# A planned attention kernel with other costs in its planner, and the last pair of heads taken head by head

## The chip, the cores and the metric

The kernel runs on one core of a Trainium2 chip. The metric is the device time of one launch in microseconds (us), as the median of several executions. A profile is one execution recorded by the hardware profiler; its span runs from the first to the last instruction and is a little shorter than the device time of the same execution.

The engines' names in the profile: PE is TensorE (matrix multiplication), PEld its weight loads, ACT is ScalarE, DVE is VectorE, POOL is GpSimd, SP issues most of the DMAs.

## The reference

Softmax attention without a mask, batch 8, 8 heads, 512 rows, 64 columns:

```python
scores = np.einsum('bhqd,bhkd->bhqk', q, k) / np.sqrt(64)
attn = np.exp(scores - scores.max(axis=-1, keepdims=True))
attn = attn / attn.sum(axis=-1, keepdims=True)
return np.einsum('bhqk,bhkd->bhqd', attn, v)
```

Inputs and output are float32, 64 heads in all.

## The kernel before

**Pairs and groups.** Heads are taken in 32 pairs, g = 0 to 31. The scores of a head are computed transposed, keys on the partitions: a chunk c of 128 keys against all 512 queries is one block of 128x512, so a pair has eight blocks (g, c, h). The list `stream` gives the order of the blocks; two successive blocks make a group m, which lies in one PSUM tile `st` of 128x1024 (three such tiles, `ps_st`). Between the first and the last pair a group is chunk c of both heads, so that pair g holds groups 4g to 4g+3. The last group is split in two, so there are 129 groups, 0 to 128.

**Stages of a pair.** SP loads k, q and v in float32. GpSimd casts them to float16 (`qkp`, line 331, and `vp`, line 323; V has an added column of ones). PE transposes q and k (eight 128x128 transposes, line 348) into one of two PSUM banks (`ps_x`, tags x0 and x1), and VectorE copies them to `tqk` (line 355, "copy"). PE then computes a group's scores, two matmuls of depth 64 (line 374): head h sits on partitions 64h to 64h+63. ScalarE takes the exponential of the whole group into `pt` (line 379). The values of a head are computed in four units, each the sum over the four chunks for 128 queries (four matmuls of 65 columns, line 462); seven units share a bank `o`. When the seven are done VectorE normalises them (a reciprocal and a multiplication, lines 440 and 441, "norm") into `ring`, and SP stores the heads that are complete (line 449).

**Groups on VectorE.** Some groups' exponentials are computed on VectorE instead of ScalarE: first a "raise" reads the scores from PSUM into integers `z` (line 393), then six passes finish the exponential from SBUF (lines 406, 417 and four times 428).

**The order.** Each engine works its instructions in the order in which the program issues them, and that order is set when the kernel is built by the class `Plan`. It runs a clock in steps of 5 ns with booked costs (the constants ahead of `__init__`), in two parts:

- `step_pe` decides for PE. If the scores of the next group may start (a PSUM tile `st` is free and the pair's copy is done: `free`), and either those of the one after could too or ScalarE's booked work (`backlog`) is under HURRY, it issues scores. If the scores aren't due but will be within 150 ns and the backlog is small, it holds PE. Otherwise it issues transposes of the next pair if their data are booked as there (`ready_kq`) and a bank is free, or a unit of values (`values`), or scores after all.
- `step_dve` decides for VectorE. A raise, copy or normalisation that is due goes first, raises ahead of the others. If none is due, the next pass goes, unless a job already known falls due more than LATE before the end of the pass.

`for_dve` says whether a group goes to VectorE: not before group 6, not in the last three pairs, and only if no pass of the group before is still to be issued and no raise waits. `exps[m]` is the booked time at which group m's exponentials are there; `values` starts a head when all its groups are. Of the last head, the values of a chunk start when that chunk is there (`wants`, `last_values`, line 477), in a bank of their own.

The first three groups are issued by `first_pair`, outside the class; the constructor books their times. The step "feed" issues the loads of pair g+5 and the casts of pairs g+3 and g+2; it goes ahead of the first scores of pair g.

Of the kernel before, what the change touches and what calls it, by code (L numbers as in the profile page):

```python
# [12 lines left out]
EXP = mybir.ActivationFunctionType.Exp  # L13
# [3 lines left out]
class Plan:  # L17
# [10 lines left out]

    SLOT, EXP, EXP_DONE, EXP_FIXED = 216, 853, 1085, 51
    INTO, OUT_OF = 95, 105
    TRANSPOSE, V_UNIT = 225, 130
    TO_ACT, TO_DVE, TO_PE = 275, 210, 60
    COPY, NORM, NORM_COLUMN = 700, 380, 67
    RAISE, PASSES, LATE = 1216, (867, 822, 1400, 1400, 1400, 1372), 700
    HURRY = 1200
    STEP = 5
    FIRST_UNIT = 4

    def __init__(self, groups, pairs, first):
        self.groups, self.pairs = groups, pairs
        self.pe, self.act, self.dve = 6000, 4800 + first * 904, 5800
        self.m, self.tiled = first, True
        self.read = []
        self.exps = {}
        for m in range(first):
            self.exps[m] = 4800 + m * 904 + self.EXP_DONE
            self.read.append(self.exps[m])
        self.tq = {0: 5800}  # L50
        self.next_t = 1
        self.part_t = 0
        self.banks = [5100, 5800]
        self.todo = [(g, h) for g in range(pairs) for h in range(2)]
        self.head = None
        self.units = self.FIRST_UNIT
        self.member = {b: m for m, grp in enumerate(groups) for b in grp}
        self.ready = []
        self.passes = []
        self.steps = []  # L60

    def note(self, t, *what):
# [15 lines left out]
    def for_dve(self, m):  # L78
        g = self.groups[m][0][0]
        return (  # L80
            m > 5
            and g < self.pairs - 3
            and not self.passes
            and not any(x[1] == "raise" for x in self.ready)
        )

    def scores(self, t):
        m, grp = self.m, self.groups[self.m]
        slots = 2 if len(grp) == 2 and 0 < grp[0][0] and grp[0][2] == grp[1][2] else 1
        on_dve = self.for_dve(m)  # L90
        if m % 4 == 0 and grp[0][0] > 0 and len(grp) == 2:
            self.note(t, "feed", grp[0][0])
        self.note(t, "scores", m, on_dve)
        t += (0 if self.tiled else self.INTO) + self.SLOT * slots
        self.tiled = True
        if on_dve:
            self.ready.append((t + self.TO_DVE, "raise", (m,)))
            self.read.append(1e9)
        else:
            begin = max(self.act, t + self.TO_ACT)  # L100
            self.act = begin + self.EXP * len(grp) // 2 + self.EXP_FIXED
            self.exps[m] = self.act + self.EXP_DONE - self.EXP - self.EXP_FIXED
            self.read.append(self.exps[m])
        self.m += 1
        self.pe = t
# [61 lines left out]
    def step_pe(self, t):  # L167
        if self.m == len(self.groups):
            self.values(t)
            return  # L170
        g = self.groups[self.m][0][0]
        backlog = self.act - t
        one, two = self.free() <= t, self.free(1) <= t
        if one and (two or backlog < self.HURRY):
            return self.scores(t)
        if not one and backlog < 1300 and self.free() < t + 150:
            return
        if self.part_t:
            return self.transposes(t)
        if (  # L180
            self.next_t < self.pairs
            and self.next_t <= g + 1
            and t >= self.ready_kq(self.next_t)
            and self.bank(t) is not None
        ):
            return self.transposes(t)
        if not self.values(t) and one:
            self.scores(t)

    def step_dve(self, t):  # L190
        now = [x for x in self.ready if x[0] <= t]
        if now:
            job = min(now, key=lambda x: (x[1] != "raise", x[0]))
            self.ready.remove(job)
            _, kind, what = job
            self.note(t, kind, *what)
            if kind == "norm":
                self.dve = t + self.NORM + self.NORM_COLUMN * what[1]
                self.banks[what[2]] = self.dve + self.TO_PE
            elif kind == "copy":  # L200
                self.dve = t + self.COPY
                self.banks[what[1]] = self.tq[what[0]] = self.dve + self.TO_PE
            else:
                self.dve = t + self.RAISE
                self.read[what[0]] = self.dve + self.TO_PE
                self.passes += [(what[0], s) for s in range(len(self.PASSES))]
        elif self.passes:
            m, s = self.passes[0]
            if min((x[0] for x in self.ready), default=1e9) > t + self.PASSES[s] - self.LATE:
                self.passes.pop(0)  # L210
                self.note(t, "pass", m, s)
                self.dve = t + self.PASSES[s]
                if s == len(self.PASSES) - 1:
                    self.exps[m] = self.dve + self.TO_PE

    def run(self):
        t = 0
# [12 lines left out]
def kernel(  # L230
# [10 lines left out]
    NI = S // P  # L241
# [4 lines left out]
    LAST = NP - 1  # L246


    stream = []
    for g in range(NP):  # L250
        if g == 0:
            stream += [(g, c, h) for h in range(2) for c in range(NI)]
        elif g == LAST:
            stream += [(g, c, h) for c in range(2) for h in range(2)]
            stream += [(g, c, h) for h in range(2) for c in range(2, NI)]
        else:
            stream += [(g, c, h) for c in range(NI) for h in range(2)]
    groups = [stream[n : n + 2] for n in range(0, len(stream), 2)]
# [31 lines left out]
    first = {}  # L290
# [310 lines left out]
    with tc.manual_schedule():  # L601
        first_loads()
        load(1, "kq")
        load(0, "v")
        for g in range(2, 5):
            load(g, "kq")
            load(g - 1, "v")
        load(4, "v")
        make_identity(nc, ident)
        for n in range(NV):  # L610
            nc.vector.memset(vps[n][:, :, :, D : D + 1], 1.0)
        first_pair()
        cast_qk(1)
        cast_v(0)
        cast_qk(2)
        cast_v(1)
        feed(0)
        do = {
            "transposes": transposes,
            "scores": scores,  # L620
            "values": values,
            "feed": feed,
            "raise": raise_,
            "copy": lambda g, b: copy(g),
            "pass": pass_,
            "norm": lambda u, n, b: normalise(u, n),
        }
        for what, *args in Plan(groups, NP, 3).run():
            do[what](*args)
# [30 lines left out]
```

## Time and profile before

| What | Value |
|---|---|
| median of 5 executions | 123.27 us (122.89 to 124.48) |
| the profiled execution: device time | 123.39 us |
| its span | 121.6 us |
| busy time of PE / DVE / ACT / POOL | 107.7 / 99.6 / 114.3 / 74.7 us |
| granted TensorE clock | 0.999 |
| groups raised on VectorE | 6 |
| first DMA issue, last DMA issue | 0.73 and 118.94 us |

A row of the group table reads: line, engine, operation, out<-in by tile names, shapes, how many | busy time, mean ns of one | the engine's idle time just before them, and what ended most of it. A row of the timeline reads: start, length, engine, line, operation, how many were merged, and in brackets the idle time ahead and its releaser. The chain of waits is followed back from the last instruction to what released each.

### The profile page before, as it was taken

How to read it: one execution, taken by the hardware profiler on the slowest of the kernel's cores; microseconds unless marked ns; L12 is line 12 of the kernel's file. 1: busy time of each engine (PE TensorE's matmuls, PEld its weight loads, DVE VectorE, ACT ScalarE, POOL GpSimd, SP SyncE). 2: the span in 40 equal slices, each digit the busy share in tenths (PEclk: the TensorE clock that was granted, in tenths of full speed). 3: DMA queues.
4: the chain of work that ended last, by engine and by line, in shares of the span. 5: the costliest groups of instructions: out<-in, count | busy, mean ns of one | idle time of the engine just before them, and what ended most of it. 6: DMA issues, size and time to landing. Idle time of an engine off the chain costs nothing.

```text
span 121.6 us, 3951 instructions
## 1 busy us (share of the span) xinstructions
PE 107.7 (89%) x1557; PEld 67.2 (55%) x1557; DVE 99.6 (82%) x171; ACT 114.3 (94%) x127; POOL 74.7 (61%) x101
## 2 busy tenths in 40 slices
PE   7969788889899798998998998889999998999970
PEld 2636455547456455664566564656655665556550
DVE  1457899989999898699999899996979899976451
ACT  4699999999999999999999999999999999999970
POOL 2358979998699958396587981465955479200000
PEclk9999999999999999999999999999999999999999
DMA  4999999999999999996899998998999893313234
GB/s 116 289 334 382 381 380 384 383 319 302 356 362 330 325 328 340 319 339 237 248 302 286 308 321 281 279 328 264 312 322 334 286 314 102 102 49 127 91 113 152
DMA packets 35603, 33.82 MB, mean 278 GB/s; under 512 B 2688, under 2 KB 35584, under 8 KB 35584
## 3 DMA queue, kind: packets, MB, share of 16 engines
q1 hardware_dynamic: 35152, 33.24, 83.8%
q10 hardware_dynamic: 432, 0.33, 0.9%
q8 instruction: 12, 0.20, 0.7%
q14 instruction: 7, 0.06, 0.1%
HBM read 25.17 MB, written 8.39 MB: 276 GB/s over the span
## 4 chain that ended last, share of the span: by engine, by line
ACT 51%; issue 23%; PE 16%; DMA 4%; SPq 1%; DVE 1%; POOL 1%; ACTq 0%
ACT pt L379 51%; PE st L374 7%; PE o L462 7%; DMA v<-in_v_dram 4%; PE tp L348 2%; SPq L318 1%; SPq L506 1%; PE o_last L477 1%; DVE ring L441 1%; POOL vp L323 1%; DVE obl L490 0%; DVE rc L440 0%; DVE rc_last L489 0%; ACTq L379 0%
## 5 line engine op out<-in xcount | busy, mean ns | idle before, releaser
L379 ACT ACTIVATE pt<-st 128x1024 f16<-128x1024 f32 (+1 forms) x120 | 109.4, 1336 | 0.4 <-PE st L374 0.4
L374 PE MATMUL st<-tqk 64*128 64x512 f16 x248 | 48.1, 384 | 6.9 <-ACT pt L379 6.4
L462 PE MATMUL o<-vp,pt 128*128 128x65 f16 x1008 | 46.9, 195 | 2.1 <-ACT pt L379 1.3
L462 PEld LDWEIGHTS <-pt 128*128 128x128 f16 x1008 | 37.0, 98 | 19.2 <-issue 15.3
L331 POOL CAST qkp<-k 128x512 f16<-128x512 f32 x31 | 25.0, 806 | 23.5 <-DMA k<-in_k_dram 14.4
L331 POOL CAST qkp<-q 128x512 f16<-128x512 f32 x30 | 25.5, 850 | 2.2 <-DMA q<-in_q_dram 2.0
L323 POOL CAST vp<-v 128x512 f16<-128x512 f32 x32 | 25.4, 796 | 0.9 <-DMA v<-in_v_dram 0.8
L374 PEld LDWEIGHTS <-tqk 64*128 64x128 f16 x248 | 13.3, 93 | 20.2 <-issue 12.2
L441 DVE TENSOR_TENSOR ring<-o,rc 128x448 f32<-128x448 f32 (+2 forms) x37 | 22.6, 612 | 1.3
L355 DVE COPY tqk<-tp 128x1024 f16<-128x1024 f16 x30 | 20.5, 684 | 2.8 <-PE tp L348 2.7
L348 PE MATMUL tp<-ident,qkp 128*128 128x128 f16 x248 | 19.7, 220 | 0.3 <-DVE ring L441 0.2
L348 PEld LDWEIGHTS <-qkp 128*128 128x128 f16 x248 | 14.0, 98 | 7.4 <-issue 5.5
L428 DVE SCALAR_TENSOR_TENSOR y<-y,m 128x1024 f32<-128x1024 f32 x12 | 16.2, 1347 | 0.0
L440 DVE RECIPROCAL rc<-o 128x7 f32<-128x7 f32 (+2 forms) x37 | 7.3, 198 | 8.8 <-PE o L462 8.7
L428 DVE SCALAR_TENSOR_TENSOR y<-m 128x1024 f32<-128x1024 f32 x6 | 8.6, 1436 | 0.0
L393 DVE TENSOR_SCALAR z<-st 128x1024 uint32<-128x1024 f32 x6 | 7.3, 1222 | 0.9 <-PE st L374 0.9
L428 DVE SCALAR_TENSOR_TENSOR pt<-y,e 128x1024 f16<-128x1024 f32 x6 | 7.9, 1309 | 0.0
L417 DVE TENSOR_SCALAR e<-z 128x1024 uint32<-128x1024 uint32 x6 | 6.1, 1021 | 0.0
L406 DVE TENSOR_SCALAR m<-z 128x1024 uint32<-128x1024 uint32 x6 | 5.0, 838 | 0.0
L510 PE MATMUL st_0a<-const-bfloat16-1.0 128*128 128x512 bf16 (+1 forms) x11 | 3.5, 482 | 0.8 <-PEq L644 0.8
L510 PEld LDWEIGHTS <-const-bfloat16-1.0 128*128 128x128 bf16 x15 | 1.7, 129 | 2.4 <-issue 2.4
L526 ACT ACT_TABLE_LOAD x1 | 1.3, 1283 | 1.7 <-PEq L644 1.7
(43 smaller groups left out, 17.6 us busy)
## 6 DMA issues: line engine op xcount, KB each, us to landing
out_dram<-ring SPq DMA_DIRECT2D x63, 128.0 KB, 3.7
k<-in_k_dram SPq DMA_DIRECT2D x31, 256.0 KB, 4.6
q<-in_q_dram SPq DMA_DIRECT2D x31, 256.0 KB, 4.8
v<-in_v_dram SPq DMA_DIRECT2D x27, 256.0 KB, 5.1
v<-in_v_dram SPq DMA_DIRECT2D x10, 128.0 KB, 3.9
k<-in_k_dram ACTq DMA_DIRECT2D x2, 128.0 KB, 2.8
q<-in_q_dram SPq DMA_DIRECT2D x2, 128.0 KB, 2.5
out_dram<-obl SPq DMA_DIRECT2D x1, 64.0 KB, 1.8
```

The costliest lines, as they stand in the source:

```text
L323: nc.gpsimd.tensor_copy(out=vps[g % NV][:, :, :, 0:D], in_=raw[g]["v"][:, :, :, :])
L331: eng.tensor_copy(out=t[:, n].rearrange("p i (h d) -> p h i d", h=2), in_=raw[g][name][:, :, :, :],)
L348: nc.tensor.transpose(tps[g][:, n, i, :], qkp[g][:, n, i, :], ident)
L355: nc.vector.tensor_copy(out=tqk[g][:, :, :], in_=tps.pop(g).rearrange("p n i c -> p n (i c)"))
L374: nc.tensor.matmul(st[:, x, :], kc, qc, start=True, stop=True)
L379: nc.scalar.activation(out=pt[:, 0:size, :], in_=st[:, 0:size, :], func=EXP, scale=scale)
L393: nc.vector.tensor_scalar(out=r["z"][:, :, :], in0=r["st"][:, :, :], scalar1=scale * 1.4426950408889634 * 2.0**23, scalar2=(127 + SHIFT) * ...
L417: nc.vector.tensor_scalar(out=r["e"][:, :, :], in0=r["z"][:, :, :], scalar1=0xFF800000, scalar2=None, op0=AluOp.bitwise_and,)
L428: nc.vector.scalar_tensor_tensor(out=r["pt"][:, :, :] if n == 3 else r["y"][:, :, :], in0=mant if n == 0 else r["y"][:, :, :], scalar=QUAR ...
L440: nc.vector.reciprocal(out=rc[:, 0:n], in_=o[:, x : x + n, D : D + 1])
L441: nc.vector.tensor_tensor(out=ring[:, u % NU : u % NU + n, :], in0=o[:, x : x + n, 0:D], in1=rc[:, 0:n].broadcast_to([P, n, D]), op=AluOp. ...
L462: nc.tensor.matmul(os[u // 7][:, u % 7, :], blocks[(g, c, h)][:, y * P : (y + 1) * P], vps[g % NV][:, h, c, :], start=(c == 0), stop=(c == ...
```

## The change

All the planner's booked costs are set anew, each VectorE cost as two numbers (how long the engine is taken, and when the result is there), the passes get a factor MARGIN of 1.1, and the rules for lateness are set by kind of job. The first exponentials are booked later, PE's and VectorE's clocks start at 7000, at most seven groups go to VectorE and none in the last four pairs, and the exponentials of a group on VectorE are booked as there 1200 ns later than its passes end. The last pair's blocks come in the order of its heads, so that its groups hold two chunks of one head instead of one chunk of both. `BY_DMA` is empty, and what depends on it does nothing; `AHEAD` is 0, which leaves the rule on passes as it was.

```diff
-    SLOT, EXP, EXP_DONE, EXP_FIXED = 216, 853, 1085, 51
+    SLOT, EXP, EXP_DONE, EXP_FIXED = 216, 853, 181, 64
     INTO, OUT_OF = 95, 105
     TRANSPOSE, V_UNIT = 225, 130
     TO_ACT, TO_DVE, TO_PE = 275, 210, 60
-    COPY, NORM, NORM_COLUMN = 700, 380, 67
-    RAISE, PASSES, LATE = 1216, (867, 822, 1400, 1400, 1400, 1372), 700
-    HURRY = 1200
+    COPY, NORM, RAISE = (615, 700), (307, 390), (1145, 1225)
+    NORM_COLUMN, PASS_DONE = 67, 80
+    PASSES = (690, 950, 1335, 1335, 1335, 1250)
+    FIRST_EXP = 5260
...
+    BY_DMA = ()
+    LATE_NORM, LATE_COPY, HURRY, SOON, BACKLOG = 400, 1400, 1400, 150, 1600
+    LAST_PAIRS, AHEAD, MARGIN, SLACK, MOST = 4, 0, 1.1, 1200, 7
...
-        self.pe, self.act, self.dve = 6000, 4800 + first * 904, 5800
+        self.pe, self.act, self.dve = 7000, self.FIRST_EXP, 7000
...
-            self.exps[m] = 4800 + m * 904 + self.EXP_DONE
+            self.act += self.EXP + self.EXP_FIXED
+            self.exps[m] = self.act + self.EXP_DONE
...
             m > 5
-            and g < self.pairs - 3
-            and not self.passes
+            and g < self.pairs - self.LAST_PAIRS
+            and len(self.passes) <= self.AHEAD
+            and len(self.on_dve) < self.MOST
...
-        if not one and backlog < 1300 and self.free() < t + 150:
+        if not one and backlog < self.BACKLOG and self.free() < t + self.SOON:
...
-                self.dve = t + self.NORM + self.NORM_COLUMN * what[1]
-                self.banks[what[2]] = self.dve + self.TO_PE
+                more = self.NORM_COLUMN * what[1]
+                self.dve = t + self.NORM[0] + more
+                self.banks[what[2]] = t + self.NORM[1] + more + self.TO_PE
...
-            if min((x[0] for x in self.ready), default=1e9) > t + self.PASSES[s] - self.LATE:
+            end = t + int(self.MARGIN * self.PASSES[s])
+            late = {"copy": self.LATE_COPY, "norm": self.LATE_NORM, "raise": self.LATE_NORM}
+            if all(x[0] > end - late[x[1]] for x in self.ready):
                 self.passes.pop(0)
                 self.note(t, "pass", m, s)
-                self.dve = t + self.PASSES[s]
+                self.dve = end
                 if s == len(self.PASSES) - 1:
-                    self.exps[m] = self.dve + self.TO_PE
+                    self.exps[m] = end + self.PASS_DONE + self.TO_PE + self.SLACK
...
-        if g == 0:
+        if g in (0, LAST):
             stream += [(g, c, h) for h in range(2) for c in range(NI)]
-        elif g == LAST:
-            stream += [(g, c, h) for c in range(2) for h in range(2)]
-            stream += [(g, c, h) for h in range(2) for c in range(2, NI)]
```

More of the change, by code (lines that the diff above doesn't have):

```diff
@@ L47, in __init__ @@
         for m in range(first):
-            self.exps[m] = 4800 + m * 904 + self.EXP_DONE
+            self.act += self.EXP + self.EXP_FIXED
+            self.exps[m] = self.act + self.EXP_DONE
             self.read.append(self.exps[m])
-        self.tq = {0: 5800}
+        self.tq = {0: 5800, **{g: 0 for g in self.BY_DMA}}
         self.next_t = 1
@@ L59, in __init__ @@
         self.passes = []
+        self.on_dve = []
         self.steps = []
@@ L96, in scores @@
         if on_dve:
+            self.on_dve.append(m)
             self.ready.append((t + self.TO_DVE, "raise", (m,)))
@@ L101, in scores @@
             self.act = begin + self.EXP * len(grp) // 2 + self.EXP_FIXED
-            self.exps[m] = self.act + self.EXP_DONE - self.EXP - self.EXP_FIXED
+            self.exps[m] = self.act + self.EXP_DONE
             self.read.append(self.exps[m])
@@ L170, in step_pe @@
             return
+        while self.part_t == 0 and self.next_t in self.BY_DMA:
+            self.next_t += 1
         g = self.groups[self.m][0][0]
@@ L197, in step_dve @@
             if kind == "norm":
-                self.dve = t + self.NORM + self.NORM_COLUMN * what[1]
-                self.banks[what[2]] = self.dve + self.TO_PE
+                more = self.NORM_COLUMN * what[1]
+                self.dve = t + self.NORM[0] + more
+                self.banks[what[2]] = t + self.NORM[1] + more + self.TO_PE
             elif kind == "copy":
-                self.dve = t + self.COPY
-                self.banks[what[1]] = self.tq[what[0]] = self.dve + self.TO_PE
-            else:
-                self.dve = t + self.RAISE
-                self.read[what[0]] = self.dve + self.TO_PE
+                self.dve = t + self.COPY[0]
+                self.banks[what[1]] = self.tq[what[0]] = t + self.COPY[1] + self.TO_PE
+            else:
+                self.dve = t + self.RAISE[0]
+                self.read[what[0]] = t + self.RAISE[1] + self.TO_PE
                 self.passes += [(what[0], s) for s in range(len(self.PASSES))]
```

## The prediction

> **What bounds the kernel now.** I read the page first (busy shares, costliest groups), then ScalarE's timeline, then VectorE's, then all engines at both ends.
>
> ```profile
> PE 107.7 (89%) x1557; PEld 67.2 (55%) x1557; DVE 99.6 (82%) x171; ACT 114.3 (94%) x127; POOL 74.7 (61%) x101
> ```
>
> The page's first part (span 121.6 us) puts ScalarE, ACT, ahead; its group rows say why. The reader is to see 0.4 us of idle ahead of the exponentials, while PE's score matmuls wait 6.4 us for them: ScalarE is waited for, and hardly waits.
>
> ```profile
> L379 ACT ACTIVATE pt<-st 128x1024 f16<-128x1024 f32 (+1 forms) x120 | 109.4, 1336 | 0.4 <-PE st L374 0.4
> L374 PE MATMUL st<-tqk 64*128 64x512 f16 x248 | 48.1, 384 | 6.9 <-ACT pt L379 6.4
> ```
>
> ScalarE's timeline (start, length, what) merges work without idle:
>
> ```profile
> 7.92 1.02 ACT L379 ACTIVATE pt<-st 128x1024 f16<-128x1024 f32 x1
> 9.36 108.33 ACT L379 ACTIVATE pt<-st 128x1024 f16<-128x1024 f32 x119 [0.42 <-PE st L374]
> ```
>
> One block of 119 exponentials, 117 of two blocks and two of one. An earlier window ends one piece after six of them: 9.36 us, 5.61 us long. Less one lone exponential (1.02), five steps make 4.59, so 0.918 each. 117 times 0.917 is 107.3; the two halves take the other 1.0. The block is therefore full pitch from 9.36 to 117.69: **nothing that only orders work better inside it can gain.** Three things can move the time: how many groups go to ScalarE, when its second exponential starts (9.36), and the 3.9 us behind its last one.
>
> VectorE's timeline, the first and last of the raises (L393) that begin a group computed there; between them lie those at 25.03, 41.38, 59.05 and 74.36:
>
> ```profile
> 11.02 1.22 DVE L393 TENSOR_SCALAR z<-st 128x1024 uint32<-128x1024 f32 x1
> ...
> 92.90 1.22 DVE L393 TENSOR_SCALAR z<-st 128x1024 uint32<-128x1024 f32 x1
> ```
>
> Six groups, 81.9 us from first to last: 16.4 us a chain.
>
> **Part 1, the new costs: how many raises?** A seventh would take one step, 0.92 us, off ScalarE; this decides the forecast. The class places a raise only when the passes of the last one are handed out, so the interval is what the plan books for VectorE. Its clock is used here for order alone; every price is from the trace.
> Before, a chain books 1216 + 867 + 822 + 3 x 1400 + 1372 = 8477 ns, a copy 700, a normalisation of seven columns 380 + 469 = 849. Between the first and last raise VectorE's timeline holds 24 copies and 25 normalisations: 5 x 8.477 + 24 x 0.700 + 25 x 0.849 = 80.4 us booked, of 81.9 elapsed. The booked line is full.
> After, a chain books 1145 + 759 + 1045 + 3 x 1468 + 1375 = 8728 (each pass times 1.1), a copy 615, a normalisation 776. The same jobs: 43.6 + 14.8 + 19.4 = 77.8 us, 0.5 us less a chain. The margins eat half of what the cheaper copies and normalisations free.
> The new limit (pairs below 28, not 29) leaves group 111 as the last that may be raised. I walked the class by hand from its start with the new constants: raises at 10.8 (group 6), 24.6 (group 22) and 40.9 us (group 41) of its clock. The second interval, 16.35 us, is one chain, five copies, five normalisations (15.68) and 0.67 of waiting, because a pass is held when a known normalisation falls due more than 400 ns ahead of the pass's end. From group 41 to 111 are 70 groups; four more raises need 17.5 a chain, of which 16.5 on ScalarE, 16.5 x 0.917 = 15.1 us. Some 17 copies and 20 normalisations fall there: 34.9 + 10.5 + 15.5 = 60.9 us, 15.2 a chain with no idle at all. With a wait like the one walked it is 15.9, 4 x 15.9 = 63.6 us against 4 x 15.1 = 60.4: the seventh candidate comes 3 us late. I take **six raises as before: ScalarE's work unchanged, 0.** Ends: 0 and -0.92 (a seventh). The cap of seven and the one-chain-at-a-time rule then change nothing.
>
> **Part 2, the start.** The timeline of all engines around the second exponential:
>
> ```profile
> 7.96 0.62 POOL L323 CAST vp<-v 128x512 f16<-128x512 f32 x1 [0.81 <-DMA v<-in_v_dram]
> 8.12 0.76 DVE L353 COPY tqk<-tp 128x512 f16<-128x512 f16 x2 [0.49 <-PE tp L348]
> ...
> 8.63 0.29 PE L462 MATMUL o<-vp,pt 128*128 128x65 f16 x4 [0.55 <-POOL vp L323]
> ...
> 8.93 0.61 PE L374 MATMUL st<-tqk 64*128 64x512 f16 x4
> ```
>
> PE's queue holds one unit of values (4 matmuls) ahead of the scores of group 4; that unit waits for V's cast until 8.58 and just ends as the copy of pair 1 ends (8.88), so today it costs some 0.05. The class puts it there because at 8300 of its clock V is booked ready, and holds PE from 8430 on since the copy is due (8525) within 150. After the change PE's clock starts at 7000 with the scores of group 3 ahead of the transposes, the copy is booked 220 later (8745), and at 8430 and 8560 it isn't yet within 150: two more units go ahead of these scores. Behind PE's head here wait the scores of groups 4 and 5, and ScalarE for them. Price: in the chain of waits a run of 12 value matmuls takes 0.49 us and a run of 4 takes 0.23, so +0.26; less the 0.05 that the copy sets anyway, **+0.2**. Ends: 0 (the order isn't as I walked it) and +0.26. Nothing covers it: ScalarE stood idle 0.42 there already, and all 119 exponentials shift.
>
> **Part 3, copies may wait behind passes (1400 late), scores sooner (1400 of backlog, not 1200).** In the walk the scores of the next pair still come at 0.7 to 1.4 us of booked ScalarE backlog; the largest delay met is pair 3's copy behind two passes. By VectorE's rows its raise starts near 11.1, the raise takes 1.25 from start to start, the passes 0.82 and 1.05, the copy 0.68: 14.9, and with 0.4 for the scores 15.3. ScalarE then has seven groups from 9.56: 9.56 + 7 x 0.917 = 16.0. Cost 0; cover: those 0.7 us. If it is gone, the shortage goes straight into the span. The V-ready and cast times, the loads' feeds and SP's and POOL's queues keep their order by pairs; 0. Values of a raised pair are booked 1200 later: PE takes other heads meanwhile, 0; it matters only where nothing else is left, at the end, and a sixth raise near 89 us (40.9 + 3 x 16) is done by about 105, sooner than now.
>
> **Part 4, last pair head by head.** The tail in the same view:
>
> ```profile
> 114.28 0.60 PE L374 MATMUL st<-tqk 64*128 64x512 f16 x2
> ...
> 116.18 1.20 PE L462 MATMUL o<-vp,pt 128*128 128x65 f16 x24
> 116.65 0.21 DVE L440 RECIPROCAL rc<-o 128x7 f32<-128x7 f32 x1 [1.53 <-PE o L462]
> 116.76 0.49 PEld L462 LDWEIGHTS <-pt 128*128 128x128 f16 x14 [0.22 <-ACT pt L379]
> 116.89 0.62 DVE L441 TENSOR_TENSOR ring<-o,rc 128x448 f32<-128x448 f32 x1
> ...
> 117.57 0.67 PE L477 MATMUL o_last<-vp,pt 128*128 128x65 f16 x16 [0.19 <-DVE ring L441]
> ```
>
> Two score matmuls of one head take 0.60 here, of two heads 0.39 elsewhere. Two more groups become one-head: 2 x 0.21 = 0.42 us of PE, while ScalarE has two groups in hand; in the path 0. Gain: head 0's values can start one group sooner (they wait 0.22 at 116.76 for an exponential). But the last head's 16 matmuls wait for the bank that the normalisation of 116.65 to 117.51 frees; that follows the last values of pair 30, whose exponentials and scores ahead keep their places. So the wait of 0.22 goes and the bank's wait grows by as much: **0**. Ends: -0.4 (0.22 and 0.19 both go) and +0.4 (the dearer scores push pair 30's values back).
>
> A rule speaks against this part: "TensorE: Matmul & The Clock Gate" of the Trainium skill, "Part 3: Packing small matmuls", has small matmuls run concurrently only where each lies in its own row group. Our 0.60 against 0.39 agrees in direction; a full doubling of 0.39 would make 0.78 us of the two groups instead of 0.42, and the sum would be the same, as both lie beside ScalarE.
>
> **Sum.** 0 + 0.2 + 0 + 0 on the profiled execution's 123.39 (span 121.6 and 1.8 around it): 123.6. That execution lies 0.12 above the median of 123.27, so 123.5.
>
> **Rivals.**
> Seven raises: the plan idles less than in the interval I walked. For it, the 60.9 us of bookings just fit; against, they fit only without any wait. 123.5 - 0.9 = 122.6, and 122.2 if the tail gains 0.4 too. A seventh raise past 101 us has its chain end some 14 us later, at about 115, so its pair's 32 value matmuls (a run of 32 takes 1.13 us in the chain of waits) may fall into the tail, giving back up to 1.1: 123.7.
> ScalarE starves behind a late copy (the other side): place, the first scores of a pair whose copy waits behind a pass, in the chains where casts on GpSimd slow the passes (1.63 us at 54.6 and 99.8 against 1.22). It decides once the copy is later than the 0.7 us of backlog; two such passes in a row run 2 x (1.63 - 1.47) = 0.32 over their booking. Once in each of six chains that is at most 1.9, and 1.2 if two chains in six are spared: 124.7 to 125.4.
> No change at all: the start is not as walked; 123.3.
>
> **How the numbers follow.** Forecast (six raises, start later by 0.2): 0.53. No change: 0.17. Seven raises: 0.15. Starving: 0.15. Measurement tells about 1% (1.2 us) from no change: below 122.0 is faster, above 124.5 slower. Faster needs a seventh raise and all of the tail's gain: 0.06. Slower is the starving: 0.15. Within: 0.79. Likeliest case alone: 123.2 to 123.8. The range reaches from seven raises (122.4) to the start of starving (124.6).
>
> **What would show it.** Count of L393: six right, seven wrong. In the timeline 12 value matmuls ahead of the first scores of pair 1, and the long ScalarE block beginning near 9.56, still one piece 108.3 long: right. More than one piece, or idle "PE st" of over 0.6 in the group row: starving. Last-head matmuls still ending about 0.55 behind the last exponential: part 4 right.

## The result, and the profile after

The changed kernel takes 123.53 us (median of 54 executions) against 123.26 (94 executions); the ratio is 1.0026, with a 95% interval of 1.0015 to 1.0036. The change costs about 0.3 us. The profiled execution took 124.38 us with a span of 122.6: TensorE's granted clock was halved in it from 116.25 us on, which most executions don't show, so it is read here up to that point (and for ScalarE's block, whose last scores are ahead of it), and a second profile (123.23 us, span 121.4, below) gives the end.

The group rows of the page, changed kernel (ScalarE's exponentials are now line 391, the scores line 386):

```profile
L391 ACT ACTIVATE pt<-st 128x1024 f16<-128x1024 f32 (+1 forms) x120 | 109.4, 1337 | 1.0 <-PE st L386 1.0
L386 PE MATMUL st<-tqk 64*128 64x512 f16 x248 | 48.4, 384 | 5.8 <-ACT pt L391 3.3
```

Still 120 exponentials and 109.4 us. ScalarE's timeline says where the idle 1.0 us is:

```profile
7.47 1.04 ACT L391 ACTIVATE pt<-st 128x1024 f16<-128x1024 f32 x1
9.48 108.34 ACT L391 ACTIVATE pt<-st 128x1024 f16<-128x1024 f32 x119 [0.97 <-PE st L386]
```

The long block is one piece of 108.34 us, as before (108.33); it starts 0.12 us later and ends at 117.82. The raises, by the rows of the tile z:

```profile
L405 DVE TENSOR_SCALAR z<-st x6: 1214/1215/1225, 11.1 to 86.4; 128x1024 uint32<-128x1024 f32 x6
```

Six, and the last 6.5 us sooner: the five intervals take 75.3 us, 15.1 each on average, where they took 16.4. The start, timeline of all engines:

```profile
7.91 0.62 POOL L335 CAST vp<-v 128x512 f16<-128x512 f32 x1 [0.73 <-DMA v<-in_v_dram]
...
8.12 0.76 DVE L365 COPY tqk<-tp 128x512 f16<-128x512 f16 x2 [0.49 <-PE tp L360]
...
8.58 0.54 PE L474 MATMUL o<-vp,pt 128*128 128x65 f16 x12 [0.49 <-POOL vp L335]
...
9.05 0.60 PE L386 MATMUL st<-tqk 64*128 64x512 f16 x4
```

Twelve value matmuls where there were four, and the scores at 9.05 instead of 8.93, although the copy ends at 8.88 in both. What is left of the 0.3 us, some 0.2, had to lie behind the last exponential or in the spread of the start. The experiments look for it, and test what a raise is worth.

### The profile page after: what moved, and what is told of

Read it like the earlier page. It is cut to its first block, busy times and chain, and to the rows that moved or that the text cites. A ratio compares the mean times of both kernels' runs of the same rounds, so it can differ in the third digit from the quotient of the medians.

```text
span 122.6 us, 3952 instructions
## 1 busy us (share of the span) xinstructions
PE 109.6 (89%) x1557; PEld 69.2 (56%) x1557; DVE 97.8 (80%) x171; ACT 114.3 (93%) x127; POOL 74.8 (61%) x101
## 4 chain that ended last, share of the span: by engine, by line
ACT 56%; issue 20%; PE 12%; DMA 4%; DVE 3%; SPq 1%; POOL 1%; ACTq 0%
ACT pt L391 56%; PE st L386 5%; PE o L474 4%; DMA v<-in_v_dram 4%; PE tp L360 1%; DVE z L405 1%; PE o_last L489 1%; SPq L330 1%; SPq L518 1%; DVE tqk L367 1%; DVE ring L453 1%; POOL vp L335 1%; DVE obl L502 0%; DVE rc L452 0%; DVE rc_last L501 0%
## 5 line engine op out<-in xcount | busy, mean ns | idle before, releaser
L391 ACT ACTIVATE pt<-st 128x1024 f16<-128x1024 f32 (+1 forms) x120 | 109.4, 1337 | 1.0 <-PE st L386 1.0
L474 PE MATMUL o<-vp,pt 128*128 128x65 f16 x1008 | 49.1, 196 | 1.7 <-ACT pt L391 0.8
L474 PEld LDWEIGHTS <-pt 128*128 128x128 f16 x1008 | 38.2, 99 | 21.1 <-issue 17.4
L343 POOL CAST qkp<-k 128x512 f16<-128x512 f32 x31 | 27.5, 887 | 23.4 <-DMA k<-in_k_dram 16.1
L335 POOL CAST vp<-v 128x512 f16<-128x512 f32 x32 | 26.5, 830 | 0.9 <-DMA v<-in_v_dram 0.7
L453 DVE TENSOR_TENSOR ring<-o,rc 128x448 f32<-128x448 f32 (+2 forms) x37 | 22.6, 612 | 1.3
L386 PEld LDWEIGHTS <-tqk 64*128 64x128 f16 x248 | 14.0, 93 | 16.5 <-issue 6.4
L343 POOL CAST qkp<-q 128x512 f16<-128x512 f32 x30 | 21.9, 730 | 1.4 <-DMA q<-in_q_dram 0.9
L440 DVE SCALAR_TENSOR_TENSOR y<-m 128x1024 f32<-128x1024 f32 x6 | 7.9, 1311 | 0.0
L429 DVE TENSOR_SCALAR e<-z 128x1024 uint32<-128x1024 uint32 x6 | 5.1, 842 | 0.0
```

The source lines that it names most:

```text
L335: nc.gpsimd.tensor_copy(out=vps[g % NV][:, :, :, 0:D], in_=raw[g]["v"][:, :, :, :])
L343: eng.tensor_copy(out=t[:, n].rearrange("p i (h d) -> p h i d", h=2), in_=raw[g][name][:, :, :, :],)
L386: nc.tensor.matmul(st[:, x, :], kc, qc, start=True, stop=True)
L391: nc.scalar.activation(out=pt[:, 0:size, :], in_=st[:, 0:size, :], func=EXP, scale=scale)
L429: nc.vector.tensor_scalar(out=r["e"][:, :, :], in0=r["z"][:, :, :], scalar1=0xFF800000, scalar2=None, op0=AluOp.bitwise_and,)
L440: nc.vector.scalar_tensor_tensor(out=r["pt"][:, :, :] if n == 3 else r["y"][:, :, :], in0=mant if n == 0 else r["y"][:, :, :], scalar=QUAR ...
```

## The experiments

The kernel before was run beside all of them; ratios are to it.

**The changed kernel again (after_again).** No edit.

> The changed kernel once more, unchanged, for a second profile. Forecast theory: six raises, the long ScalarE block from about 9.48 us, 108.3 us long, and at a full clock the tail behind it as long as before (3.9 us), so a span of about 121.75 and a time 0.1 above the kernel before. Rival (the tail itself became longer by its order): the tail stays at 4.1 us or more although the granted clock is 0.99 or higher. Measured ratio so far 1.0026, that is 0.32 us, of which the start explains 0.12.

123.65 us, ratio 1.0026 (1.0005 to 1.0048), as before. Of the expectation the start came out otherwise, and the tail is the rival's. All engines at the start, second profile:

```profile
6.82 0.62 POOL L335 CAST vp<-v 128x512 f16<-128x512 f32 x1 [0.79 <-DMA v<-in_v_dram]
...
7.49 0.54 PE L474 MATMUL o<-vp,pt 128*128 128x65 f16 x12
...
7.69 0.76 DVE L365 COPY tqk<-tp 128x512 f16<-128x512 f16 x2 [0.92 <-PE tp L360]
7.84 109.42 ACT L391 ACTIVATE pt<-st 128x1024 f16<-128x1024 f32 x120
```

V came 1.1 us sooner, so the twelve matmuls were done at 8.03, ahead of the copy's end (8.45), and cost nothing: the block is one piece of 120 from 7.84. So the price of the start is not fixed; it depends on when V's first load lands, and in the profiles of this case the cast of it starts anywhere from 6.82 to 8.16 us. The end of the same profile:

```profile
116.32 0.21 DVE L452 RECIPROCAL rc<-o 128x7 f32<-128x7 f32 x1 [1.63 <-PE o L474]
116.56 0.62 DVE L453 TENSOR_TENSOR ring<-o,rc 128x448 f32<-128x448 f32 x1
...
117.33 0.65 PE L489 MATMUL o_last<-vp,pt 128*128 128x65 f16 x16 [0.54 <-DVE rc L452]
```

ScalarE ends at 117.26. The reciprocal that frees the bank starts 0.94 ahead of that (1.04 before), the last head's matmuls start 0.07 behind it (0.12 ahead before), and from ScalarE's end to the span's end, the tail, it is 4.14 us, not 3.91: 0.23 more, in one execution, with the clock full until PE is done.

**The last pair alone (before_heads).** The kernel before with the new order of the last pair:

```diff
-        if g == 0:
+        if g in (0, LAST):
             stream += [(g, c, h) for h in range(2) for c in range(NI)]
-        elif g == LAST:
-            stream += [(g, c, h) for c in range(2) for h in range(2)]
-            stream += [(g, c, h) for h in range(2) for c in range(2, NI)]
```

> The kernel before with only the last pair's blocks taken head by head; planner costs as before. Forecast theory (part 4): 0 within 0.1 us, because the last head's matmuls still wait for the bank that the normalisation frees. Rival (dearer one-head score matmuls push pair 30's values back): +0.15 to +0.4 us, all behind the last exponential; if this is the missing 0.2 us of the change, it shows here.

124.04 us, ratio 1.0070 (1.0043 to 1.0097): 0.86 slower by the ratio, 0.75 by the medians, more than the whole change and more than either expectation. PE's timeline:

```profile
116.00 0.37 PE L371 MATMUL st<-tqk 64*128 64x512 f16 x1 [0.31 <-ACT pt L376]
116.31 1.45 PE L459 MATMUL o<-vp,pt 128*128 128x65 f16 x40
...
118.30 0.65 PE L474 MATMUL o_last<-vp,pt 128*128 128x65 f16 x16 [0.54 <-DVE rc L437]
```

Here 40 value matmuls (24 in the kernel before) stand behind the scores of the last half group, and those wait 0.31 us for a PSUM tile that ScalarE still reads. So the normalisation slips, and the last head starts 0.45 behind ScalarE's end (117.85); the tail is 4.45 us, 0.54 longer. The profiled execution took 124.11 us, 0.72 more than that of the kernel before; the other 0.16 lies ahead of ScalarE's end (117.85 against 117.69), where one execution differs from the next, so 0.54 is what this profile shows for the order.

**All but the last pair (after_pairs).** The changed kernel with the old order of blocks; the class then needs one guard, or it would begin the last head too soon:

```diff
+                if (g, h) == (self.pairs - 1, 1) and len(self.todo) > 1:
+                    continue
```

> The changed kernel with only the last pair's blocks in the order of before (and the last head held back until it is the only one left, which the class needs then). In the two profiles of the changed kernel at a full clock in the last microseconds the tail from the last exponential's end to the end of the span is 4.1 us against 3.9 before. Theory now (the last pair's order is what the tail lost): the tail is 3.9 again and 0.2 us are gained against the change, ratio to before about 1.001. Rival (the new costs made the tail longer, not the order of the blocks): tail 4.1, ratio to before 1.003.

123.57 us, ratio 1.0031 (1.0003 to 1.0059). The time is the rival's, but its interval holds the theory's 1.001 too, so an effect of the order under some 0.3 us would not show here. ScalarE's block, then the tail:

```profile
9.73 108.34 ACT L396 ACTIVATE pt<-st 128x1024 f16<-128x1024 f32 x119 [0.61 <-PE st L391]
```

```profile
117.12 0.21 DVE L457 RECIPROCAL rc<-o 128x7 f32<-128x7 f32 x1 [1.62 <-PE o L479]
...
118.05 0.67 PE L494 MATMUL o_last<-vp,pt 128*128 128x65 f16 x16 [0.28 <-DVE ring L458]
```

The tail is 4.03 us, between the theory's 3.9 and the rival's 4.1. The reciprocal starts 0.95 ahead of ScalarE's end (118.07), as in the changed kernel (0.94) and not as before (1.04), and 28 value matmuls stand behind the last scores in both, where there were 24: some 0.1 of the 0.23 stays with the new costs. The last head starts 0.07 behind the end of the normalisation, as before (0.06) and not as in the changed kernel (0.15): some 0.1 goes with the order of the blocks. These are differences of single profiles. That the tail is longer shows in more of them: 4.06 and 4.08 us in after_start1 and after_start2 below, which have the changed kernel's last stage, and 3.90 in before_start3, which has that of before.

**The start undone, twice (after_start1, after_start2), and done alone (before_start3).** The list that the class returns is edited, nothing else. In the first, value units 5 and 6 go right behind the scores of group 4; in the second they and their normalisation behind those of group 5; in the third, on the kernel before, they go ahead of group 4's. The first run's edit:

```diff
+        steps = Plan(groups, NP, 3).run()
+        early = [s for s in steps if s[0] == "values" and s[4] in (5, 6)]
+        steps = [s for s in steps if s not in early]
+        n = [s[:2] for s in steps].index(("scores", 4))
+        steps[n + 1 : n + 1] = early
-        for what, *args in Plan(groups, NP, 3).run():
+        for what, *args in steps:
```

> The changed kernel with its order kept, but for two value units (eight matmuls) that are taken from ahead of the scores of group 4 and put right behind them. Forecast theory (part 2): the second exponential starts at 9.36 instead of 9.48, 0.12 us are gained and the rest of the order shifts with it: -0.12. Rival (the start is hidden by slack later in the block): 0.

> The changed kernel with two value units and their normalisation taken from ahead of the scores of groups 4 and 5 to right behind both, as in the kernel before, so that PE does not change between score and value matmuls more often than there. Forecast theory (part 2): where V's cast is late (ends after 8.5 us) the long block starts 0.12 us earlier, where it is early nothing changes; over many executions 0.05 to 0.12 us gained, ratio to before about 1.002. Rival (taking them early helps, since it leaves PE fewer changes of kind and lets the raise of group 6 start sooner): 0 to 0.5 us lost.

> The kernel before with two value units (eight matmuls) taken from behind the scores of groups 4 and 5 to ahead of group 4's; all else as it was. Forecast theory (part 2): where V's cast is late the long block of exponentials starts up to 0.26 us later, else nothing: 0.05 to 0.2 us lost. Rival: 0, or a gain, because the values then run while PE would wait for the copy anyway.

The first took 124.32 us, ratio 1.0105 (1.0066 to 1.0143), the second 124.15, 1.0079 (1.0052 to 1.0106), the third 123.42, 1.0014 (0.9989 to 1.0039). Putting the units back made things worse by about 1 us, against what I expected and beyond the rivals. The second run, timeline of all engines:

```profile
9.32 0.56 PE L474 MATMUL o<-vp,pt 128*128 128x65 f16 x12
...
10.01 0.36 DVE L453 TENSOR_TENSOR ring<-o,rc 128x192 f32<-128x192 f32 x1
...
10.51 0.61 PE L360 MATMUL tp<-ident,qkp 128*128 128x128 f16 x8 [0.63 <-DVE ring L453]
...
11.69 2.88 ACT L391 ACTIVATE pt<-st 128x1024 f16<-128x1024 f32 x3 [0.54 <-PE st L386]
```

In the new order the next transposes use the bank that these units' normalisation frees (in the old order they use the other one). With the units late the transposes wait 0.63, the scores behind them come late, and ScalarE stands idle 0.54 at group 7. So this edit doesn't measure the start alone; it shows that the units' place and the choice of bank belong together. The third run does: 0.14% with 0 in the interval, in line with a small price and not proof of it.

The profiles say more. Six of them have twelve value matmuls ahead of the first scores of pair 1. Where V's cast ends 0.29 to 0.36 us ahead of the copy's end (after, after_pairs, seven_105), these scores start 0.17 to 0.23 behind it; where the cast ends 0.50 to 1.01 ahead (after_again, after_margin1, seven_copy700), they start 0.04 or 0.05 behind it. In the kernel before, with four matmuls and V's cast 0.30 ahead, it is 0.05. So the start costs 0.12 to 0.18 where V is that late, and nothing where it is earlier.

**One raise fewer (before_five).** In the kernel before:

```diff
-            and g < self.pairs - 3
+            and g < 24
```

with the guard of above. 

> The kernel before without its sixth raise (no group of pair 24 or later goes to VectorE, and the last head is held back until it is the only one left): five groups on VectorE instead of six. Forecast theory (ScalarE's block has no idle, so each group is worth one step): +0.92 us, 124.2. Rival (the last chain on VectorE crowds the end, so leaving it out gives some back): +0.3 to +0.6.

124.36 us, ratio 1.0100 (1.0067 to 1.0133), 0.8 to 1.6 us: the theory's 0.92 lies in it, the rival's 0.3 to 0.6 doesn't. ScalarE's timeline:

```profile
8.21 110.33 ACT L381 ACTIVATE pt<-st 128x1024 f16<-128x1024 f32 x121
```

121 exponentials in 110.33 against 120 in 109.42: one raise is 0.91 us of block. The rest of the loss is the tail, 4.16 us against 3.91; whether the guard or the missing raise made it longer wasn't separated.

**Seven raises.** Margin 1.0 instead of 1.1 (after_margin1):

```diff
-    LAST_PAIRS, AHEAD, MARGIN, SLACK, MOST = 4, 0, 1.1, 1200, 7
+    LAST_PAIRS, AHEAD, MARGIN, SLACK, MOST = 4, 0, 1.0, 1200, 7
```

> The changed kernel with the factor on the passes at 1.0 instead of 1.1. Forecast theory (part 1: the booked length of a chain sets how many groups are raised, and each is worth one step of ScalarE): seven raises, the last near 95 us; ScalarE's block is 107.4 us long, and the time falls by 0.92 us to about 122.6. Rival (passes without margin run late in the real order and ScalarE starves behind them, or the seventh chain's values crowd the tail): seven raises, but ScalarE's block in several pieces or a tail of more than 4.5 us, and a time of 123.5 or more.

124.09 us, ratio 1.0067 (1.0040 to 1.0094): the rival. ScalarE's timeline falls into four pieces:

```profile
7.80 14.89 ACT L391 ACTIVATE pt<-st 128x1024 f16<-128x1024 f32 x16
22.87 32.40 ACT L391 ACTIVATE pt<-st 128x1024 f16<-128x1024 f32 x35 [0.19 <-PE st L386]
55.55 11.31 ACT L391 ACTIVATE pt<-st 128x1024 f16<-128x1024 f32 x12 [0.28 <-PE st L386]
67.17 50.59 ACT L391 ACTIVATE pt<-st 128x1024 f16<-128x1024 f32 x56 [0.31 <-PE st L386]
```

119 exponentials, one fewer, yet from 7.80 to 117.76 is 109.96 us, and the tail is 4.6 us. What happened before the third piece, VectorE's timeline and then PE's:

```profile
49.15 1.51 DVE L440 SCALAR_TENSOR_TENSOR pt<-y,e 128x1024 f16<-128x1024 f32 x1
50.59 1.21 DVE L405 TENSOR_SCALAR z<-st 128x1024 uint32<-128x1024 f32 x1
51.72 0.68 DVE L367 COPY tqk<-tp 128x1024 f16<-128x1024 f16 x1
```

```profile
52.45 0.61 PE L386 MATMUL st<-tqk 64*128 64x512 f16 x2 [0.62 <-DVE tqk L367]
```

The transposes of that copy ended by 49.0; the copy waits behind a pass and the next raise until 51.72, and the next pair's scores 0.62 for it. From 49.6 on PE did only score matmuls, two pairs of which waited 0.53 each for ScalarE. Busy time by stretch, with the granted clock behind the five engines (PE first):

```profile
50.00:51.00 1.00, 0.40 (x3) 0.10 (x2) 1.00 (x2) 1.00 (x2) 1.00 (x1) 1.00 0.98 345
51.00:52.00 1.00, 0.39 (x2) 0.09 (x1) 1.00 (x2) 1.00 (x3) 0.45 (x2) 1.00 1.14 393
52.00:53.00 1.00, 0.55 (x3) 0.12 (x3) 0.97 (x3) 1.00 (x2) 1.00 (x3) 0.72 1.03 352
53.00:54.00 1.00, 1.00 (x8) 0.44 (x6) 1.00 (x3) 1.00 (x2) 0.44 (x1) 0.50 1.00 344
```

Behind two microseconds with PE 40% busy the clock is halved, from 52.4 to 55.8; the same score pair takes 0.61 instead of 0.39, and ScalarE runs dry at 55.27. The breaks at 22.7 and 66.9 come at a full clock.

Then copies at most 700 late (seven_copy700):

```diff
-    LATE_NORM, LATE_COPY, HURRY, SOON, BACKLOG = 400, 1400, 1400, 150, 1600
+    LATE_NORM, LATE_COPY, HURRY, SOON, BACKLOG = 400, 700, 1400, 150, 1600
```

> As the run with the factor on the passes at 1.0 (seven raises, ratio to before 1.007, ScalarE's block in four pieces), with one thing more: copies may fall due only 700 ns, not 1400, before the end of a pass. Theory (ScalarE starved there because copies waited behind passes: PE's scores waited 0.6 us for a copy at 52.4, and TensorE's granted clock fell to 0.5 meanwhile): the block is in one or two pieces, and 0.5 us or more are gained against that run, ratio 1.000 to 1.003. Rival (passes booked without a margin run late whatever waits behind them): still three or more pieces, ratio 1.006 or more.

123.92 us, ratio 1.0063 (1.0042 to 1.0084). The block is in two pieces as the theory had it (the break at 22.6 stays), but the time is the rival's: the tail is 4.8 us. Half of each. So two more, seven_pairs and seven_105, both also with the old order of the last pair and the guard (the lines replaced are those of the changed kernel):

```diff
 seven_pairs
+    LATE_NORM, LATE_COPY, HURRY, SOON, BACKLOG = 400, 700, 1400, 300, 1300
+    LAST_PAIRS, AHEAD, MARGIN, SLACK, MOST = 4, 0, 1.0, 600, 7
 seven_105
+    LATE_NORM, LATE_COPY, HURRY, SOON, BACKLOG = 800, 1400, 1400, 150, 1300
+    LAST_PAIRS, AHEAD, MARGIN, SLACK, MOST = 4, 0, 1.05, 600, 7
```

> The changed kernel with the last pair's blocks in the order of before (last head held back until it is the only one left), factor 1.0, copies at most 700 ns late, values of raised pairs booked 600 instead of 1200 ns later, PE held up to 300 ns for scores at a backlog under 1300: seven raises, the last at 97 us. Theory (a seventh raise is worth one step, 0.92 us, if nothing starves): ScalarE's block 107.4 us long, 122.5 us, ratio 0.994 to 0.998. Rival (VectorE is too full for seven chains: 104 us busy): pieces in the block and a later tail eat it, ratio 1.000 to 1.006.

> As the run before it, but factor 1.05, normalisations at most 800 ns late, copies 1400, PE held 150 ns: seven raises, the last at 98.7 us. Theory: margins of 5% keep ScalarE fed, the block is in one or two pieces, but the last chain ends near 112 us and its pair's values crowd the tail by some 0.5 us: ratio 0.997 to 1.001. Rival (late copies starve ScalarE even so): three or more pieces, ratio 1.003 to 1.008.

> The seven-raise version with the last pair in the order of before once more, to see whether its gain holds: a first series gave a ratio of 0.9972 with an interval of 0.9945 to 1.0000. Theory (one step of ScalarE gained, some of it given back at the ends): 0.995 to 0.999 again, upper end of the interval below 1.000 or close to it. Rival (the first series was luck): 1.000 or more.

seven_105: 123.54 us, ratio 1.0026 (1.0006 to 1.0047). Its block is whole, ScalarE is done at 116.51, and the end is PE's:

```profile
114.97 1.58 PE L479 MATMUL o<-vp,pt 128*128 128x65 f16 x44
116.70 0.67 PE L479 MATMUL o<-vp,pt 128*128 128x65 f16 x16 [0.15 <-DVE ring L458]
117.50 0.66 PE L494 MATMUL o_last<-vp,pt 128*128 128x65 f16 x16
```

Sixty value matmuls are left at 114.97, with those of the seventh chain's pair among them (its last pass starts at 111.06); the last head starts 0.99 behind ScalarE's end, and the tail of 5.1 us eats the raise.

seven_pairs: 122.80 us, ratio 0.9972 (0.9945 to 1.0000), and in a second series 122.86 us, 0.9985 (0.9958 to 1.0012). Its block:

```profile
8.24 108.50 ACT L396 ACTIVATE pt<-st 128x1024 f16<-128x1024 f32 x119
```

One piece, 0.92 shorter than the 120 of the other kernels, and a tail of 4.26. By its medians it is the fastest version here; both intervals reach to no change. It differs from the changed kernel in five constants and the order of the last pair, and which of them keeps the block whole wasn't tested one by one.

## Why the prediction was right, step by step

- **Six raises: right, by less than I thought.** The walk's raises at 10.8, 24.6 and 40.9 of the plan's clock stand at 11.13, 24.51 and 40.59 in the trace. From there I counted 15.9 us a chain, with the one wait I had walked (0.67); the next three intervals take 15.3 each. The last chain's last pass starts at 101.57, and group 111's scores at 100.69: the seventh candidate came 0.9 us too late, not 3. (The rival's 60.9 us of bookings against 60.4 did not quite fit even without a wait.) The margins' share was told wrong as well: 1.1 books 688 ns more a chain, 3.4 us over five, nearly all of the 3.9 us that the cheaper copies and normalisations free; what was left came from the raises and passes themselves, booked 2.2 us cheaper.
- **A raise is worth 0.92: right.** 0.91 (before_five) and 0.92 (seven_pairs) of block.
- **The start, +0.2: direction right, size a coin.** 0.12 to 0.18 in the profiles where V's cast is late, 0 in the others. I took a wait for V's cast from one execution and treated it as fixed; what I missed is that the load's landing moves by over a microsecond between executions. The 0.05 that I charged to today's unit is no cost of it: the scores follow the copy by that much where nothing stands between.
- **Copies behind passes, 0: right.** The copy that I put at 14.9 ends at 14.81, PE waits 1.17 for it, and ScalarE's block has no break. My sign for starving, idle "PE st" of over 0.6 in the group row, does show (1.0), but 0.97 of it lies ahead of the second exponential; the sign should have left the start out.
- **The last pair, 0: not measurable in the time, but wrong as a step.** Beside the old costs it costs 0.86, 0.54 of it seen in the tail (before_heads); beside the new nothing that the time shows, some 0.1 in the tail. The step that pair 30's exponentials and the scores ahead keep their places failed: in before_heads a score waiting for its PSUM tile held 40 value matmuls. The end I gave this step, +0.4, was too narrow. Its sign failed too: the last head's matmuls end 0.72 behind the last exponential (after_again) and not 0.55; 0.65 of that is there with the old order (after_pairs).
- **The sum, 123.5 against 123.53**, is partly luck: 0.2 was given to the start, and the profiles show 0 to 0.18 there and 0.15 to 0.23 in the tail, where I had 0. A third term wasn't in the sum at all: the drop of the clock described below. Without the six executions that have it the median is 123.45.
- **The rivals.** Seven raises and starving can come together: with margin 1.0 alone they did, 124.09. They need not: seven_pairs has seven raises and one unbroken block. (Of the two slow passes that priced the starving, the one at 54.6 took 1.60 us, not 1.63.)

## What to carry to other kernels

Where one engine runs without a break, count its instructions first: a better model of the other engines can move only its start, its count and what comes behind it. A planner's margin is paid in the count (1.1 cost the seventh group), and its absence can be paid in breaks (after_margin1), though not always (seven_pairs); before taking either, look at what is queued behind the instruction that would be late. An edit of the last stage must be timed under the costs it will run with, since its price here went from 0.86 to nothing that the time shows.

## What the hardware showed beside that

- The granted clock can fall in mid-kernel: in after_margin1 it is 0.50 from 52.4 to 55.8 us, behind 2 us with PE 40% busy. The changed kernel's first profile has 0.50 from 116.25 on; from 113 to 116 PE ran 27 matmuls there, and 42 in the kernel before, which kept its clock. But from 14 to 15 us PE was 13% busy in the same profile without a drop, so what share, over what time, brings it on isn't shown.
- Of the changed kernel's 54 executions 6 have a mean clock under 0.985; their median is 124.35 us, that of the others 123.45. In the 92 executions of the kernel before that ran beside the experiments none is under 0.99. With the old order of the last pair (after_pairs) it is 2 of 12, so the order of the blocks alone doesn't make it.
- "TensorE: Matmul & The Clock Gate" of the Trainium skill, Part 1, has a free-running window of about 3.4 us that judges how busy PE was. The 3.4 us of the drop in after_margin1, and that only some executions of one kernel fall into it, agree.
- Why the last head's matmuls start 0.15 behind the end of the normalisation that frees their bank in the profiles with the head-by-head order, and 0.05 to 0.07 behind it in those with the old order, stays open; it is some 0.1 us.
